# Attention scores with full-height low-part products, and value products in alternating column halves

## The chip, the cores and the metric

The kernel runs on one core of a Trainium2 chip. The metric is the device time of one execution in microseconds (us); lower is better. Engines are named as in the profile: PE (TensorE), PEld (its weight loads), DVE (VectorE), ACT (ScalarE), POOL (GpSimd), SP (SyncE, which issues transfers).

## The reference, cut to what matters

The whole program is two networks, one after the other, on 256 tokens of width 1024. The second one's first layer is an attention with 16 query heads and 4 key heads of width 64. It is computed twice: for 256 context tokens that see themselves, and for the 256 tokens of the sequence, whose keys are the context's and their own (within a window of 128). Each softmax has one extra logit per head, the sink.

```python
def block(n):
    ...
    s_ctx = jnp.einsum('bqgrd,bkgd->bgrqk', qb, kc).astype(F32) * scale
    s_win = jnp.einsum('bqgrd,bkgd->bgrqk', qb, kb).astype(F32) * scale
    s_win = jnp.where(valid, s_win, -jnp.inf)
    p = softmax_with_sink(jnp.concatenate([s_ctx, s_win], axis=-1), sink).astype(v.dtype)
    ...
...
sc = jnp.einsum('bqgrd,bkgd->bgrqk', qc, kc).astype(F32) * scale
pc = softmax_with_sink(sc, sink).astype(vc.dtype)
oc = jnp.einsum('bgrqk,bkgd->bqgrd', pc, vc).reshape(b, C, Q_DIM)
```

## The kernel before, in words

Activations lie with channels on the 128 partitions. Most products split both operands into a high part that PE multiplies in its fast fp32 form (F32R) and a low remainder, and add three products (`mm3`, L185 to L187). Weights stream through a ring of four buffers; ACT makes their high part (L57), DVE the low part (L58).

`attend` (L1405) does one attention. It loops over j (2 pairs of key heads), rp (2 pairs of query heads each) and t (2 blocks of 128 queries), so it has 8 passes of t. In a pass, e is the key head of the pair, and its data lie on partition half `HS[e]`; c is one of two query heads. A pass first makes the scores of four heads (e, c). In the context stage (`nk` is 2: 256 keys) a score is one plain fp32 product on the 64 partitions of its half (L1399); in the main stage (`nk` is 4: 512 keys, two key sets) each is two F32R products per key set (L1402, L1403). For these `q_parts` (L1384) lays the query's high part on half e and its low part on the other half, and `k_parts` (L1332) lays the keys' high part `kh[e]` on both halves; the full-height L1402 thus adds high x high and low x high. The keys' low part `kl` lies on half e alone, so L1403 runs on 64 rows.

Then comes the softmax: mask (main stage, L1431), row maximum (L1434, L1437), exponential on ACT (L1448), the sink's term and the sum (L1449 to L1452), scaling (L1455). After it each head's probabilities are transposed on PE (L1466) into an accumulator bank `ps_pt`, copied by ACT (L1468) into `at`, and multiplied with the values (L1471), which fill the column half `HS[e]` of `po`. All four heads go in the order e, then c; `at` has two buffers in both stages. A plain fp32 product shows as two instructions in the trace, a transpose and an F32R product as one.

PSUM has eight banks in four pools: scores come from `pa` (three), `ps_pt` from `pl` (two). In the main stage `po` has a bank of its own; in the context stage it takes one of the two of `pl`. In the pass with t equal to 1, the next pair's query projection (`q_proj`, L1371, tile `ps_q`) is issued between the softmax and the transposes; its rotary embedding (`rope`, `q_parts`) stands before the last two heads.

The order on each engine is made at build time: a scheduler takes the ready instruction that was written earliest, by its own estimate of durations, so that instructions written later, such as query projections and state tiles, fill waits. On the chip each engine runs that fixed order, and waits where the data isn't there.

After the main stage, `ctx_ssm` (L1664) makes start states of the next layer for groups 1 to 5. Each scales transposed inputs on DVE into the buffer `xd` (L1676 to L1678), which four fp32 products read (L1687). `xd` has `NXD` buffers, two here.

Of the kernel before, what the change touches and what calls it, by code (L numbers as in the profile page):

```python
# [8 lines left out]
F32 = mybir.dt.float32  # L9
F32R = mybir.dt.float32r  # L10
I32 = mybir.dt.int32
AF = mybir.ActivationFunctionType
ALU = mybir.AluOpType

P = 128
S = 256
# [28 lines left out]
HS = slice(0, 64), slice(64, 128)  # L45
# [22 lines left out]
class Core:  # L68
# [25 lines left out]
    TAIL = 4  # L94
    WT = 2
    NXB = 8
    NXD = 2
    UPTO = (6, 11)
    ADA = (1.0, 0.6)
    RATES = (2.4,1.6)  # L100
# [1016 lines left out]
class Second(Core):  # L1117
# [214 lines left out]
    def k_parts(self, kv, name):  # L1332

        nc = self.nc
        kh = [self.w2("%s_h%d" % (name, e), [P, 2, S], F32R) for e in range(2)]
        kl = self.w2(name + "_l", [P, 2, S], F32R)
        for e in range(2):
            for o in (e, 1 - e):
                nc.scalar.copy(kh[e][HS[o]], kv[HS[e]])
            nc.vector.tensor_tensor(kl[HS[e]], kv[HS[e]], kh[e][HS[e]].bitcast(F32), op=ALU.subtract)  # L1340
        return kh, kl

    def kv_proj(self, x, rope, q=None):
# [50 lines left out]
    def scores(self, out, q, k, e, c, j, t, parts):  # L1394

        mm = self.nc.tensor.matmul
        ts = slice(t * P, (t + 1) * P)
        if not parts:
            mm(out, q[HS[e], c, ts], k[HS[e], j], start=True, stop=True)  # L1399
            return  # L1400
        kh, kl = k
        mm(out, q[e][:, c, ts], kh[e][:, j], start=True, stop=False)  # L1402
        mm(out, q[e][HS[e], c, ts], kl[HS[e], j], start=False, stop=True)  # L1403

    def attend(self, x, kvs, rope, out, q):  # L1405

        nc = self.nc
        mm = nc.tensor.matmul
        nk = 2 * len(kvs)
        for j in range(2):  # L1410
            o = self.b4([P, 4, S], F32R, "oh"), self.b4([P, 4, S], F32R, "ol")
            out.append(o)
            for rp in range(2):
                po = self.psum.tile([P, 2, 2, P], F32, tag="pd", name="ps_o2", bufs=1) if rope else self.pl([P, 2, 2, P], "ps_o2")
                i0 = 8 * j + 4 * rp
                for t in range(2):
                    yield
                    mx, sums, nb, es = (self.sm(4, n) for n in ("at_mx", "at_sm", "at_nb", "at_es"))
                    sc = []
                    for e in range(2):  # L1420
                        if nk == 2:
                            pl2 = self.pss([P, 2, S], "ps_s")
                            pl = [pl2[:, c] for c in range(2)]
                        else:
                            pl = [self.pss([P, 512], "ps_s") for _ in range(2)]
                        for c in range(2):
                            for i, kv in enumerate(kvs):
                                self.scores(pl[c][:, i * S:(i + 1) * S], q, kv[0], e, c, j, t, rope)
                            if rope:
                                pb = S + (1 - t) * P  # L1430
                                nc.vector.tensor_tensor(pl[c][:, pb:pb + P], pl[c][:, pb:pb + P], self.amask[:, t], op=ALU.add)  # L1431
                        X = mybir.AxisListType.X
                        if nk == 2:
                            nc.vector.tensor_reduce(mx[:, 2 * e:2 * e + 2], pl2, axis=X, op=ALU.max)  # L1434
                        else:
                            for c in range(2):
                                nc.vector.tensor_reduce(mx[:, 2 * e + c:2 * e + c + 1], pl[c], axis=X, op=ALU.max)  # L1437
                        es_ = slice(2 * e, 2 * e + 2)
                        ks = slice(i0 + 2 * e, i0 + 2 * e + 2)
                        nc.vector.scalar_tensor_tensor(nb[:, es_], mx[:, es_], -0.125, self.nsink[:, ks], op0=ALU.mult, op1=ALU.min)  # L1440
                        if nk == 2:
                            s2 = self.sc([P, 2, S])
                            s_ = [s2[:, c] for c in range(2)]
                        else:
                            s_ = [self.w2("sc", [P, 512], bufs=self.NSC) for _ in range(2)]
                        for c in range(2):
                            k = 2 * e + c
                            nc.scalar.activation(s_[c], pl[c], AF.Exp, bias=nb[:, k:k + 1], scale=0.125, accum_out=sums[:, k:k + 1])  # L1448
                        nc.vector.tensor_tensor(es[:, es_], nb[:, es_], self.sink[:, ks], op=ALU.add)  # L1449
                        nc.scalar.activation(es[:, es_], es[:, es_], AF.Exp)  # L1450
                        nc.vector.tensor_tensor(sums[:, es_], sums[:, es_], es[:, es_], op=ALU.add)
                        nc.vector.reciprocal(sums[:, es_], sums[:, es_])  # L1452
                        for c in range(2):
                            k = 2 * e + c
                            nc.vector.tensor_scalar(s_[c], s_[c], sums[:, k:k + 1], None, op0=ALU.mult)  # L1455
                        sc.append(s_)
                    yield
                    if t == 1 and 2 * j + rp < 3:
                        q = self.q_proj(x, *divmod(2 * j + rp + 1, 2), rope)
                    for e in range(2):  # L1460
                        if e == 1 and t == 1 and 2 * j + rp < 3 and rope:
                            q = self.q_parts(q)
                        for c in range(2):
                            pt = self.pl([P, nk, P], "ps_pt")
                            for kb in range(nk):
                                nc.tensor.transpose(pt[:, kb], sc[e][c][:, kb * P:(kb + 1) * P], self.ident)  # L1466
                            at = self.tl([P, nk, P], name="at") if nk == 2 else self.w2("at", [P, nk, P], bufs=self.NAT)
                            nc.scalar.copy(at, pt)  # L1468
                            for kb in range(nk):
                                g = 2 * j + e  # L1470
                                mm(po[HS[e], c, t], kvs[kb // 2][1][:, kb % 2, g * 64:(g + 1) * 64], at[:, kb], start=(kb == 0), stop=(kb == nk - 1))  # L1471
                yield
                rs = slice(2 * rp, 2 * rp + 2)
                self.split(o[0][:, rs].rearrange("p r s -> p (r s)"), o[1][:, rs].rearrange("p r s -> p (r s)"), po.rearrange("p c t i -> p (c t i)"))
# [189 lines left out]
    def ctx_ssm(self, g):  # L1664
# [8 lines left out]
        for t in range(2):  # L1673
            for c, src in enumerate((xa, xb)):
                te.transpose(px[:, t, c * P:(c + 1) * P], src[:, t * P:(t + 1) * P], self.ident)
        xc = self.w2("xd", [P, 2, 2, S], bufs=self.NXD)  # L1676
        for t in range(2):
# [204 lines left out]
    def run2(self, x, out):  # L1882
# [18 lines left out]
        with ExitStack() as ctx0:  # L1901
# [4 lines left out]
            with ExitStack() as cx:  # L1906
                self.scratch(cx, 1)
                self.pool2 = cx.enter_context(self.tc.tile_pool(name="ssm", bufs=1))
                self.NXB, self.NXD = 12, 1
                self.ssm_setup(self.pool2)  # L1910
# [202 lines left out]
```

## Time and profile before

| | |
|---|---|
| median of 3 runs | 2513.29 us (2512.29 to 2518.58) |
| the profiled execution | 2511.67 us |
| its span, first to last instruction | 2509.7 us |
| mean granted clock of PE in it | 0.975 |

An instruction's line number is that of the kernel before. In a timeline the first number is the start in us from the span's start, the second the duration, and xN the count of like instructions merged into one row. PE is pipelined: an instruction's duration holds a latency that the next one overlaps, so what one costs PE is the step from its start to the next one's.

### The profile page before, as it was taken

To read this page: it belongs to the slowest core of one execution; us is meant where nothing else is said; L and a number is where in the kernel's file an instruction comes from. 1 tells how busy PE (TensorE), PEld (TensorE's weight loads), DVE (VectorE), ACT (ScalarE), POOL (GpSimd) and SP (SyncE) were. 2 spreads that over 40 slices of the span, in tenths; PEclk is the share of its full clock that TensorE was granted. 3 is DMA by queue.
4 is the path that set the end of the run, shared out by engine and by line. 5 is a ranking of instruction groups with operands and counts; after the bars stand their busy time and mean duration, and the time that the engine had idled before them with its cause. 6 is when DMAs were issued, how large, how long until landed. Compare 5 with 4: busy or idle time off the path is not lost.

```text
span 2509.7 us, 49557 instructions
## 1 busy us (share of the span) xinstructions
PE 2359.1 (94%) x19082; PEld 2072.0 (83%) x19082; DVE 1811.0 (72%) x3981; ACT 1234.1 (49%) x2615; POOL 388.9 (15%) x376
## 2 busy tenths in 40 slices
PE   7899999999998999999999999899899989989998
PEld 5787777788888887788988898778799889977997
DVE  7768876677567868687778756856666688985666
ACT  3334435554554444344555455555555556654554
POOL 4210210122013100200012202200200232232000
PEclk8999999999999999999999999899999999999999
DMA  8744563465666654464555666412566644436664
GB/s 243 227 145 148 170 168 85 135 188 186 187 200 195 181 161 140 144 207 146 175 148 179 186 185 198 109 34 85 153 185 183 174 122 126 127 102 205 207 184 130
DMA packets 513005, 404.93 MB, mean 161 GB/s; under 512 B 49969, under 2 KB 445025, under 8 KB 512001
## 3 DMA queue, kind: packets, MB, share of 16 engines
q1 hardware_dynamic: 511536, 397.41, 53.6%
q0 software_dynamic: 1232, 4.36, 0.6%
q8 instruction: 150, 2.46, 0.4%
q14 instruction: 87, 0.70, 0.1%
HBM read 393.19 MB, written 8.52 MB: 160 GB/s over the span
## 4 chain that ended last, share of the span: by engine, by line
PE 70%; DVE 16%; DMA 5%; issue 4%; ACT 4%; POOL 1%; SPq 0%; DVEq 0%; ACTq 0%; POOLq 0%
PE ps_fg L185 4%; PE ps_fg L187 4%; PE ps_fg L186 4%; PE ps_acc L186 4%; PE ps_acc L187 4%; PE ps_acc L185 4%; DVE wl L58 3%; DMA wr<-in_w_in_dram 3%; PE ps_up L187 2%; PE ps_up L186 2%; PE ps_up L185 2%; PE ps_o L1471 2%; PE acc L186 2%; PE acc L187 2%; PE acc L185 2%
## 5 line engine op out<-in xcount | busy, mean ns | idle before, releaser
L57 ACT CAST wh<-wr 128x512 fp32r<-128x512 f32 (+1 forms) x1212 | 741.4, 620 | 808.5 <-PE ps_fg L186 166.6
L58 DVE TENSOR_TENSOR wl<-wr,wh 128x512 fp32r<-128x512 f32 x1092 | 776.5, 719 | 405.6 <-ACT wh L57 398.8
L58 POOL TENSOR_TENSOR wl<-wr,wh 128x512 fp32r<-128x512 f32 (+1 forms) x120 | 160.0, 1352 | 804.1 <-ACT wh L57 789.2
L187 PE MATMUL ps_fg<-xh,wl 128*128 128x256 f32 x672 | 190.2, 283 | 0.0
L186 PE MATMUL ps_fg<-xl,wh 128*128 128x256 f32 x672 | 190.2, 283 | 0.0
L185 PE MATMUL ps_fg<-xh,wh 128*128 128x256 f32 x672 | 190.1, 283 | 0.0
L186 PE MATMUL ps_acc<-wl,hh 128*128 128x512 f32 x432 | 171.6, 397 | 8.9 <-DVE wl L58 8.9
L185 PE MATMUL ps_acc<-wh,hh 128*128 128x512 f32 x432 | 171.0, 396 | 0.0
L187 PE MATMUL ps_acc<-wh,hl 128*128 128x512 f32 x432 | 170.9, 396 | 0.0
L187 PE MATMUL ps_up<-xh,wl 128*128 128x256 f32 x480 | 135.9, 283 | 0.4 <-POOL wl L58 0.4
L185 PE MATMUL ps_up<-xh,wh 128*128 128x256 f32 x480 | 135.8, 283 | 0.0
L186 PE MATMUL ps_up<-xl,wh 128*128 128x256 f32 x480 | 135.8, 283 | 0.0
L185 PEld LDWEIGHTS ps_fg<-xh,wh 128*128 128x128 f32 x672 | 129.0, 192 | 0.4
L186 PEld LDWEIGHTS ps_fg<-xl,wh 128*128 128x128 f32 x672 | 129.0, 192 | 0.4
L187 PEld LDWEIGHTS ps_fg<-xh,wl 128*128 128x128 f32 x672 | 129.0, 192 | 0.0
L186 PEld LDWEIGHTS ps_acc<-wl,hh 128*128 128x128 f32 x432 | 81.8, 189 | 29.4 <-DVE wl L58 12.0
L185 PE MATMUL ps_fg<-ch,wh 128*128 128x256 f32 x352 | 103.1, 293 | 0.6 <-ACT wh L57 0.6
L187 PE MATMUL ps_fg<-ch,wl 128*128 128x256 f32 x352 | 101.4, 288 | 0.0
L186 PE MATMUL ps_fg<-cl,wh 128*128 128x256 f32 x352 | 101.1, 287 | 0.0
L185 PE MATMUL ps_gl<-xh,wh 128*128 128x256 f32 x336 | 99.4, 296 | 0.1
L186 PE MATMUL ps_gl<-xl,wh 128*128 128x256 f32 x336 | 97.9, 291 | 0.0
L187 PEld LDWEIGHTS ps_acc<-wh,hl 128*128 128x128 f32 x432 | 81.7, 189 | 18.9 <-DVE hl L263 0.2
(656 smaller groups left out, 6723.7 us busy)
## 6 DMA issues: line engine op xcount, KB each, us to landing
wr<-in_w_in_dram SPq DMA_DIRECT2D x110, 512.0 KB
adw<-in_ada_w_dram SPq DMA_DIRECT2D x96, 512.0 KB
wr<-in_ssm_w_in_dram SPq DMA_DIRECT2D x72, 512.0 KB
wr<-in_ffn_w_gate_dram SPq DMA_DIRECT2D x66, 512.0 KB
wr<-in_ffn_w_up_dram SPq DMA_DIRECT2D x66, 512.0 KB
wr<-in_ffn_w_down_dram SPq DMA_DIRECT2D x66, 512.0 KB
wr<-in_w_up_dram SPq DMA_DIRECT2D x64, 512.0 KB
wr<-in_w_down_dram SPq DMA_DIRECT2D x64, 512.0 KB
```

What stands on the lines that cost most here:

```text
L57: nc.scalar.copy(hi, raw[:, i:i + self.n])
L58: z = (nc.gpsimd if core.spare > 0 else nc.vector).tensor_tensor(lo, raw[:, i:i + self.n], hi.bitcast(F32), op=ALU.subtract)
L185: mm(out, ah, bh, start=first, stop=False)
L186: mm(out, ah, bl, start=False, stop=False)
L187: mm(out, al, bh, start=False, stop=last)
L1471: mm(po[HS[e], c, t], kvs[kb // 2][1][:, kb % 2, g * 64:(g + 1) * 64], at[:, kb], start=(kb == 0), stop=(kb == nk - 1))
```

## The change

`k_parts` makes the low part for each e on both partition halves, so there are two `kl` tiles per key set instead of one, and two more subtractions per call. The second score product becomes full-height, and so also adds low x low, which was left out before. Room for the tiles is taken from `xd`, which gets one buffer. In the context stage the scores go in the order c, then e, into two accumulators taken together. In both stages the transposes, copies and value products go in the order c, then e, and the value products of the two e are written alternately, after both copies.

```diff
-    NXD = 2
+    NXD = 1
...
-        kh = [self.w2("%s_h%d" % (name, e), [P, 2, S], F32R) for e in range(2)]
-        kl = self.w2(name + "_l", [P, 2, S], F32R)
+        kh, kl = ([self.w2("%s_%s%d" % (name, z, e), [P, 2, S], F32R) for e in range(2)] for z in "hl")
         for e in range(2):
             for o in (e, 1 - e):
                 nc.scalar.copy(kh[e][HS[o]], kv[HS[e]])
-            nc.vector.tensor_tensor(kl[HS[e]], kv[HS[e]], kh[e][HS[e]].bitcast(F32), op=ALU.subtract)
+                nc.vector.tensor_tensor(kl[e][HS[o]], kv[HS[e]], kh[e][HS[e]].bitcast(F32), op=ALU.subtract)
...
         mm(out, q[e][:, c, ts], kh[e][:, j], start=True, stop=False)
-        mm(out, q[e][HS[e], c, ts], kl[HS[e], j], start=False, stop=True)
+        mm(out, q[e][:, c, ts], kl[e][:, j], start=False, stop=True)
...
                     sc = []
+                    if nk == 2:
+
+                        pls = [self.pss([P, 2, S], "ps_s") for _ in range(2)]
+                        for c in range(2):
+                            for e in range(2):
+                                self.scores(pls[e][:, c], q, kvs[0][0], e, c, j, t, rope)
                     for e in range(2):
                         if nk == 2:
-                            pl2 = self.pss([P, 2, S], "ps_s")
+                            pl2 = pls[e]
...
-                            for i, kv in enumerate(kvs):
-                                self.scores(pl[c][:, i * S:(i + 1) * S], q, kv[0], e, c, j, t, rope)
+                            if nk > 2:
+                                for i, kv in enumerate(kvs):
+                                    self.scores(pl[c][:, i * S:(i + 1) * S], q, kv[0], e, c, j, t, rope)
...
-                    for e in range(2):
-                        if e == 1 and t == 1 and 2 * j + rp < 3 and rope:
+                    for c in range(2):
+                        if c == 1 and t == 1 and 2 * j + rp < 3 and rope:
                             q = self.q_parts(q)
-                        for c in range(2):
+                        ats = []
+                        for e in range(2):
                             pt = self.pl([P, nk, P], "ps_pt")
                             for kb in range(nk):
                                 nc.tensor.transpose(pt[:, kb], sc[e][c][:, kb * P:(kb + 1) * P], self.ident)
                             at = self.tl([P, nk, P], name="at") if nk == 2 else self.w2("at", [P, nk, P], bufs=self.NAT)
                             nc.scalar.copy(at, pt)
-                            for kb in range(nk):
+                            ats.append(at)
+
+                        for kb in range(nk):
+                            for e in range(2):
                                 g = 2 * j + e
-                                mm(po[HS[e], c, t], kvs[kb // 2][1][:, kb % 2, g * 64:(g + 1) * 64], at[:, kb], start=(kb == 0), stop=(kb == nk - 1))
+                                mm(po[HS[e], c, t], kvs[kb // 2][1][:, kb % 2, g * 64:(g + 1) * 64], ats[e][:, kb], start=(kb == 0), stop=(kb == nk - 1))
```

## Rows read from the trace of the kernel before

**Rows 1.** The page, part 1: busy time, share of the span, instructions.

```profile
PE 2359.1 (94%) x19082; PEld 2072.0 (83%) x19082; DVE 1811.0 (72%) x3981; ACT 1234.1 (49%) x2615; POOL 388.9 (15%) x376
```

**Rows 2.** The page, part 4: the chain that ended last, by engine.

```profile
PE 70%; DVE 16%; DMA 5%; issue 4%; ACT 4%; POOL 1%; SPq 0%; DVEq 0%; ACTq 0%; POOLq 0%
```

**Rows 3.** Busy time by engine in the main and the context stage.

```profile
core 0: us, PE busy (x) PEld busy (x) DVE busy (x) ACT busy (x) POOL busy (x), PEclk, DMA share, GB/s
1605.00:1738.00 133.00, 132.12 (x841) 105.53 (x842) 85.56 (x225) 71.34 (x170) 6.99 (x5) 1.00 0.23 57
391.00:463.00 72.00, 70.12 (x430) 50.06 (x429) 40.89 (x134) 41.05 (x138) 0.00 (x0) 0.98 0.32 78
```

**Rows 4.** Waits, 1608 to 1735: who waited for whom, us, times, longest.

```profile
DVE ps_s L1431 <- PE ps_s L1403: 29.2, 26, 3.5
...
PEld ps_o L1471 <- ACT z_at L1468: 1.5, 6, 0.3
```

**Rows 5.** Waits, 388 to 466, the context stage.

```profile
DVE at_mx L1434 <- PE ps_s L1399: 11.1, 10, 2.1
...
PEld ps_o L1471 <- ACT at L1468: 6.3, 15, 0.7
```

**Rows 6.** Timeline of PE, 1621.4 to 1628.5 (main stage).

```profile
1621.47 0.39 PE L1402 MATMUL ps_s<-z_kc_h,z_qs 128*128 128x256 f32 x1 [0.29 <-ACT z_sc L1448]
...
1623.98 1.12 PE L1326 MATMUL ps_qp<-q,c_perm 128*128 128x512 f32 x2
...
1625.06 1.04 PE L1466 MATMUL ps_pt<-c_first,z_sc 128*128 128x128 f32 x8
...
1626.34 1.96 PE L1471 MATMUL ps_o<-z_at,kv 128*64 128x128 f32 x16
1628.23 0.38 PE L1402 MATMUL ps_s<-z_kc_h,z_qs 128*128 128x256 f32 x1
```

**Rows 7.** Timeline of PE, 1611 to 1615: query products, full height, same size.

```profile
1614.78 0.28 PE L187 MATMUL ps_q<-xh,wl 128*128 128x256 f32 x1
1614.90 0.28 PE L185 MATMUL ps_q<-xh,wh 128*128 128x256 f32 x1
```

**Rows 8.** Timeline of PE, 1655 to 1672: a short run of value products.

```profile
1661.92 1.09 PE L1471 MATMUL ps_o<-z_at,kv 128*64 128x128 f32 x8
```

**Rows 9.** Timeline of PE, 406.8 to 411.7 (context stage).

```profile
406.87 0.70 PE L1399 MATMUL ps_s<-kv,q 64*128 64x256 f32 x2
407.49 0.65 PE L1471 MATMUL ps_o<-at,kv 128*64 128x128 f32 x4
408.07 0.44 PE L1466 MATMUL ps_pt<-c_first,sc 128*128 128x128 f32 x2
408.44 0.70 PE L1399 MATMUL ps_s<-kv,q 64*128 64x256 f32 x4
409.07 0.65 PE L1471 MATMUL ps_o<-at,kv 128*64 128x128 f32 x4
```

**Rows 10.** Timeline of PE, 394.5 to 396.5: four score instructions of one head.

```profile
394.94 1.13 PE L1399 MATMUL ps_s<-kv,q 64*128 64x256 f32 x4 [0.96 <-ACT sc L1448]
396.00 0.39 PE L186 MATMUL ps_q<-cl,wh 128*128 128x256 f32 x1
```

**Rows 11.** Timeline of PE, 1123.3 to 1124.2: a modulation product in four column groups.

```profile
1123.49 0.64 PE L1160 MATMUL ps_ada<-adw,csc 128*32 128x256 f32 x8
1124.06 0.34 PE L586 MATMUL ps_l<-w_AR,w_Bn 64*64 64x128 f32 x4
```

**Rows 12.** Line 1340, the keys' low part: ns min/median/max, first and last start.

```profile
L1340 DVE TENSOR_TENSOR z_kc_l<-kc,z_kc_h x2: 684/687/690, 1322.9 to 1324.1; 64x512 fp32r<-64x512 f32 x2
L1340 DVE TENSOR_TENSOR z_k_l<-k,z_k_h x2: 677/683/689, 1616.2 to 1618.0; 64x512 fp32r<-64x512 f32 x2
```

**Rows 13.** Groups by line, 1600 to 1740: busy us, mean ns, idle before.

```profile
L1468 ACT COPY z_at<-ps_pt 128x512 f32<-128x512 f32 x32 | 17.1, 589 | 16.1 <-PE ps_pt L1466 16.1
```

**Rows 14.** Timeline of all engines, 1736 to 1751: the buffer xd.

```profile
1738.64 1.46 PE L1687 MATMUL ps_h<-z_xd,cBt 128*128 128x256 f32 x6
...
1740.36 1.29 DVE L1649 TENSOR_TENSOR z_xd<-ps_xct,wctx 128x512 f32<-128x512 f32 x2 [1.66 <-PE ps_xct L1675]
```

## Prediction

> **What bounds the kernel now.** I began with the page: TensorE (PE) is busy for 94% of the span [rows 1], and the chain of work that ended last runs through PE for 70% of it [rows 2]. So work taken off PE can shorten the kernel, if the stage it is taken from is itself held by PE. The change touches two stages, the attention of the context (391 to 463 us) and the main one (1605 to 1738 us). The table by stretches shows what limits each: in the main one PE is busy 132.1 of 133 us, DVE 85.6, ACT 71.3; in the context PE 70.1 of 72, DVE 40.9, ACT 41.1 [rows 3]. The waits say the same from the other side: in the main stage DVE sits 29.2 us until the second score product (L1403) is done, PE's weight loads only 1.5 us for the copied probabilities [rows 4]; in the context DVE waits 11.1 us for scores, and PE's loads 6.3 us for copies, so there PE is already partly held by the chain [rows 5]. Last, the timeline of PE, read by starts and not by durations: the time from one start to the next is what an instruction costs PE, its duration holds pipeline latency too.
>
> **The change part by part.**
>
> *Scores, main stage.* Today a full-height product (L1402) alternates with one on 64 rows (L1403). Eight of them take 1621.47 to 1623.98, 2.51 us, 0.314 us each [rows 6]. A full-height product of the same 256 columns in a stream of its like starts 0.12 us after the one before [rows 7]. The change makes every second product full-height, so the stream never changes its shape: 128 products (8 passes of t, 4 heads, 2 key sets, 2 products) x 0.194 = 24.8 us. Some already stand next to products of their own height, so I take 23 (estimate).
>
> *Values, main stage.* A run of 16 instructions, which is two heads in one column half (each fp32 product is two instructions, and L1471 has 256 of them for 128 products), takes PE 1.89 us, from 1626.34 to 1628.23 [rows 6]. A run of eight is 0.87 shorter, 1.96 against 1.09 [rows 8], so it costs 1.02. The passes show one run of 16 and two of eight: 3.93 us, 31.4 over 8 passes. After the change each pass has two runs of 8 + 8 in the two column halves. No row shows 64-wide column halves side by side. The nearest is the modulation product, in four column groups of 32 and also two instructions per product: its eight instructions take 0.57 us from start to the next engine start [rows 11], while two 256-column instructions in one place, one after the other, take 0.63 [rows 9]. Four groups thus cost no more than one. With that, 16 instructions cost little more than a run of eight, 1.02; I take 1.06, 17.0 over the stage's 16 runs: 14.4 saved. The bounds: 0 if the halves don't overlap, 14.4 if they do fully. I take 14.4, the modulation product being the same kind of packing.
>
> One rule speaks against this. The Trainium skill, page "TensorE: Matmul & The Clock Gate", section "What overlaps and what doesn't", says that a weight load overlaps with running products only when its row group differs; the two column halves share all their rows. By that rule this saving would be about 0, as in the first rival below. [rows 11] disagree with it.
>
> *Values, context.* A run of four costs 0.58 us (407.49 to 408.07) [rows 9], 32 runs, 18.6 us. Joined in pairs, 16 runs at a little more, 0.61: 9.8, so 8.8 saved.
>
> *Scores, context.* Four instructions in both row halves cost 0.63 us (408.44 to 409.07), as much as two in one half (406.87 to 407.49) [rows 9], while four in one half cost 1.06 [rows 10]. So row halves do overlap, and PE does it today wherever the two happen to be adjacent. Per two passes of t today: five such runs at 0.63, 3.15 us, 12.6 over the stage. After: each pass all eight in pairs, 1.06 (the row of four singles, doubled up), 8.5. Saved 4.1.
>
> In sum PE loses 37.4 us of work in the main stage and 12.9 in the context, 50.3.
>
> *What of it reaches the end, main.* With 132.1 - 37.4 = 94.7 us of PE work left, DVE's 85.6 comes close, and the softmax between scores and values alternates DVE and ACT. No row shows this stage with DVE so loaded. Bounds: it could follow PE fully (95 us, DVE at 0.90) or stay where DVE is used as now, 0.64, and gain nothing. I take DVE at 0.82, nearer to the full end because DVE's largest waits there are the 29.2 us for the products that shrink: (85.6 + 1.4) / 0.82 = 106 us, a gain of 27. The transfers won't hold it up: the DMA share there is 0.23 [rows 3].
>
> *What reaches the end, context.* Transposes and the accumulator share two PSUM buffers here, so the second head's transposes wait until the first head's copy has read the buffer, and now the values wait for both copies. Bounds 0 and 12.9; PE already waits there [rows 5], so I take half, 6.5.
>
> *Added subtractions.* Each call of k_parts gets two more on half the partitions, 0.683 us each [rows 12]. The context keys' pair is made at 1323 [rows 12], 280 us ahead of the stage that reads it. The own keys' pair stands just ahead of the first scores, where PE has query products to run: between 0 and 1.4, taken as 1.4 (also in the 87 above).
>
> *One xd buffer instead of two.* The next group's scaling (L1649) must now wait until the last group's products are through. It does so already: the products that read the buffer start their last run at 1738.64 and the next scaling starts at 1740.36, just when its own input is transposed [rows 14]. Cost 0; if groups overlapped more, at most 1.29 us per group, 6.5 for five.
>
> *Added waits.* The values of the first head wait for the copy of the second, 0.589 us later [rows 13]; behind them in PE's queue stand the next scores, and the next copies wait for the two probability buffers, both held until the pair is through. In the main stage the next pass's scores and query products cover this; without that cover it costs 0.59 x 16 = 9.4.
>
> Sum: -27 - 6.5 + 1.4 + 0 = -32. The profiled execution took 2511.7 (span 2509.7), 1.6 below the median of 2513.3: 2481 us as a median.
>
> **The rivals.**
> *Column halves don't overlap.* For it: the column halves share rows, and the scheduler may put all of one head's values first. Against: [rows 11]. Then PE frees 23 in the main stage (110 us left, above the 106) and 4.1 in the context, half of it felt: -23 - 2 + 1.4, 2490. Chance 0.15.
> *The softmax chain takes over early.* DVE can't be filled beyond 0.70 because both heads' softmax stands before the first values: 87 / 0.70 = 124 us, -9, context 0, +1.4: 2506. For it: PE's loads in the context wait for copies already [rows 5]. Against: DVE's own waits end mostly with PE. Chance 0.12.
> *Everything freed is felt.* -50, 2463, if queries and the context's next work fill each gap. Chance 0.10.
> *Lost overlap, slower.* Today the first head's transposes, copies and values run while the second head's softmax is on DVE. Afterwards no values run until both are done, and only two probability buffers exist. If this phase lies bare, each pair costs eight transposes (1.04) [rows 6], two copies (2 x 0.589) [rows 13] and its values (1.06), 3.3 us, 52 over the 16 pairs, against 37.4 freed; with 1.4 for the subtractions and the context taken as even, +16: 2529. It decides from 4.7 us of bare wait per main pass (37.4 / 8); today it is 1.5 us in the whole stage [rows 4]. Chance 0.08.
>
> **How the numbers follow.** The forecast of a 32 us gain has 0.55, its own range 2471 to 2494 (DVE share 0.76 to 0.88, context 0 to 10). The range for all runs from full effect (2463) to the early chain (2505), leaving out the slower case and part of the early chain. About 0.3%, 7.5 us, is what a measurement can tell from no change, so below 2506 is faster: the forecast, the full case, the column rival and a third of the chain case, 0.84; within 0.3% 0.08; slower 0.08.
>
> **What the changed profile would show.** Right: the L1402/L1403 products start 0.12 us apart, with the weight load of L1403 on 128 rows; the values' instructions start in pairs some 10 ns apart and 16 of them take about 1.06 us; the main stage is near 106 us with DVE above 0.8 and DVE's wait for scores well under 29 us, PE's wait for DVE or ACT grown to some 10 us; the context stage near 66 us. Wrong: values still at 0.11 us each; PE idle of over 4.7 us per main pass before transposes or values; DVE share as before at a shorter PE; or a gain there that comes back as a wait for weights or in the state groups after 1735.

## The result, and the profile after

The changed kernel took 2483.13 us (median of four runs, 2480.52 to 2488.66), the kernel before 2515.88 beside it: a ratio of 0.9874, 95% interval 0.985 to 0.9898, so 32.7 us faster. Measured a second time it took 2479.57 against 2511.0: 0.9885, interval 0.9862 to 0.9908. Its profiled execution took 2480.52 us, with a span of 2478.6 and a mean granted clock of 0.974.

The page of the changed kernel, part 1, which answers to [rows 1]:

```profile
PE 2327.0 (94%) x19082; PEld 2050.7 (83%) x19082; DVE 1813.5 (73%) x3985; ACT 1235.4 (50%) x2615; POOL 388.4 (16%) x376
```

PE lost 32 us of busy time, as much as the whole kernel became shorter, and its weight loads 21; DVE, ACT and POOL kept theirs within 2.5 us. The instruction counts of PE are the same; DVE has the four subtractions more. Where the time went is read by stretches. The next two fences give the main stage from its first score product to its last value product, before and after; the columns are those of [rows 3], with all instructions in the first row, then only those that touch the scores' accumulators, the value products' and the query projection's (`ps_s`, `ps_o`, `ps_q`). Before:

```profile
1611.20:1733.80 122.60, 121.72 (x765) 95.86 (x764) 78.39 (x212) 65.01 (x158) 5.70 (x4) 1.00 0.22 57
1611.20:1733.80 122.60, 40.37 (x128) 23.49 (x128) 31.02 (x64) 23.66 (x64) 1.00 0.22 57
1611.20:1733.80 122.60, 32.78 (x255) 27.23 (x256) 2.08 (x3) 1.76 (x3) 1.00 0.22 57
1611.20:1733.80 122.60, 24.87 (x144) 18.96 (x144) 0.00 (x0) 1.76 (x3) 1.00 0.22 57
```

After:

```profile
1608.80:1702.10 93.30, 89.82 (x755) 76.57 (x754) 80.13 (x214) 65.61 (x158) 5.76 (x4) 1.00 0.27 69
1608.80:1702.10 93.30, 23.11 (x128) 17.53 (x128) 30.26 (x64) 23.75 (x64) 1.00 0.27 69
1608.80:1702.10 93.30, 24.01 (x255) 16.53 (x256) 2.06 (x3) 1.75 (x3) 1.00 0.27 69
1608.80:1702.10 93.30, 22.16 (x144) 18.74 (x144) 0.00 (x0) 1.76 (x3) 1.00 0.27 69
```

The stage is 29.3 us shorter, nearly the whole gain. PE's busy time in it fell by 31.9: 17.3 for the scores, 8.8 for the values, 2.7 for the query products, which nobody touched, and 3.2 for the rest. The stage has ten instructions fewer, all of them state products (`ps_xbc`, 96 before, 86 after) that now run elsewhere, so some 2 us of the 29.3 are moved and not saved. PE still fills 96% of the stage, and DVE 80.1 of 93.3 us, 0.86. The waits of the same stage, which answer to [rows 4]:

```profile
DVE ps_s L1437 <- PE ps_s L1402: 5.2, 6, 1.7
...
PEld ps_o L1481 <- ACT z_at L1475: 2.0, 8, 0.4
```

DVE's wait for scores shrank from 29.2 to 5.2 us, and the weight loads wait hardly more for the copied probabilities, 2.0 us against 1.5. The timeline of PE shows the two edits at work, and one flaw (x14 stands for 14 instructions in one row):

```profile
1620.08 0.28 PE L1402 MATMUL ps_s<-z_kc_l,z_qs 128*128 128x256 f32 x1
1620.20 0.28 PE L1401 MATMUL ps_s<-z_k_h,z_qs 128*128 128x256 f32 x1
1620.32 0.28 PE L1402 MATMUL ps_s<-z_k_l,z_qs 128*128 128x256 f32 x1
...
1623.21 0.43 PE L1481 MATMUL ps_o<-z_at,kv 128*64 128x128 f32 x2
1623.57 0.39 PE L187 MATMUL ps_q<-xh,wl 128*128 128x256 f32 x1
...
1628.78 1.09 PE L1481 MATMUL ps_o<-z_at,kv 128*64 128x128 f32 x14
1629.80 0.66 PE L1473 MATMUL ps_pt<-c_first,z_sc 128*128 128x128 f32 x4
```

Score products now follow each other at 0.12 us whether high or low part, where [rows 6] had 0.314. Of the 16 instructions of a value run, two go alone ahead of the rest (here by 5.6 us, elsewhere in the stage by 0.7 to 3.8): the first head's first product, ready as soon as its own copy is. The other 14 take 1.02 us to the next start; most of them begin in pairs 7 ns apart. All 16 value runs of the stage look like this.

The context stage, first score to last value product, with all instructions, scores, values. Four profiles have the context in the order of before. In three of them (the kernel before and two experiments below, from 396.6, 398.0 and 393.2) the granted clock stands at 0.5 for 3.4 us of the stage, and it takes about 70.7 us. I take the fourth, the experiment on xd below, where it stands at 1.00 throughout:

```profile
394.40:463.60 69.20, 67.31 (x422) 47.88 (x422) 40.47 (x133) 40.09 (x135) 0.00 (x0) 1.00 0.32 80
394.40:463.60 69.20, 13.62 (x64) 6.60 (x64) 11.04 (x16) 17.34 (x64) 1.00 0.32 80
394.40:463.60 69.20, 20.52 (x127) 13.03 (x128) 2.04 (x3) 1.78 (x3) 1.00 0.32 80
```

The changed kernel:

```profile
393.60:461.40 67.80, 67.35 (x425) 46.39 (x424) 38.89 (x133) 40.40 (x136) 0.00 (x0) 1.00 0.34 83
393.60:461.40 67.80, 15.99 (x64) 8.03 (x64) 10.76 (x16) 16.64 (x64) 1.00 0.34 83
393.60:461.40 67.80, 17.08 (x128) 9.60 (x128) 2.05 (x3) 1.76 (x3) 1.00 0.34 83
```

Only 1.4 us came of it, and none of that is work taken off PE, which is busy for 67.3 us in both. The values lost 3.4 us of PE time, but the scores cost 2.4 more. The timeline says why:

```profile
407.41 0.43 PE L1481 MATMUL ps_o<-at,kv 128*64 128x128 f32 x2
407.77 0.70 PE L1398 MATMUL ps_s<-kv,q 64*128 64x256 f32 x2
408.40 0.65 PE L1481 MATMUL ps_o<-at,kv 128*64 128x128 f32 x6
408.98 0.44 PE L1473 MATMUL ps_pt<-c_first,sc 128*128 128x128 f32 x2
```

A value run is broken into 2 + 6, for 0.36 and 0.58 us to the next start, and two score instructions go alone for 0.63, the price of four in both row halves [rows 9].

### The profile page after: what moved, and what is told of

It reads as the page before. It is cut to its first block, busy times and chain, and to the rows that moved or that the text cites. A ratio compares the mean times of both kernels' runs of the same rounds, so it can differ in the third digit from the quotient of the medians.

```text
span 2478.6 us, 49551 instructions
## 1 busy us (share of the span) xinstructions
PE 2327.0 (94%) x19082; PEld 2050.7 (83%) x19082; DVE 1813.5 (73%) x3985; ACT 1235.4 (50%) x2615; POOL 388.4 (16%) x376
## 4 chain that ended last, share of the span: by engine, by line
PE 69%; DVE 17%; DMA 5%; issue 4%; ACT 4%; POOL 1%; SPq 0%; ACTq 0%; DVEq 0%; POOLq 0%
PE ps_fg L185 5%; PE ps_fg L187 4%; PE ps_fg L186 4%; PE ps_acc L186 4%; PE ps_acc L187 4%; PE ps_acc L185 4%; DVE wl L58 4%; DMA wr<-in_w_in_dram 3%; PE ps_up L187 2%; PE ps_up L186 2%; PE ps_up L185 2%; PE acc L185 2%; PE acc L186 2%; PE acc L187 2%; PE ps_o L1481 2%
## 5 line engine op out<-in xcount | busy, mean ns | idle before, releaser
L186 PEld LDWEIGHTS ps_acc<-wl,hh 128*128 128x128 f32 x432 | 81.6, 189 | 27.8 <-DVE wl L58 10.3
```

Source lines behind the costliest of these rows:

```text
L186: mm(out, ah, bl, start=False, stop=False)
```

## The experiments

All times are medians; each ratio is to the kernel before on the same chip.

**Scores alone.** The changed kernel with the value order, and the order of the context scores, as before.

```diff
-                    for c in range(2):
-                        if c == 1 and t == 1 and 2 * j + rp < 3 and rope:
+                    for e in range(2):
+                        if e == 1 and t == 1 and 2 * j + rp < 3 and rope:
...
```

> The change with its order of scores and values undone: only the full-height second score product of the main stage (and one xd buffer) is left. The main stage, first score product to last value product, took 122.6 us before and 93.3 with the whole change. Theory (PE held the main stage, and each of the two parts frees its own PE time; with both, DVE at 0.84 takes back some 8 us): the scores alone free 23, the stage takes 99 to 102 us, the run is 20 to 23 us faster than before, the values stay at 0.109 us an instruction. Rival (the chain of softmax and copies holds the stage, and it is the new order of the values that loosened it): the stage stays above 110 us and the gain below 12. The context stage stays at 70 to 71 us in both.

2497.42 us, ratio 0.9935, interval 0.9912 to 0.9959. Main stage, all instructions, scores, query products:

```profile
1612.60:1716.50 103.90, 100.32 (x766) 88.73 (x764) 79.57 (x214) 65.06 (x158) 5.75 (x4) 1.00 0.26 66
1612.60:1716.50 103.90, 22.80 (x128) 17.56 (x128) 30.47 (x64) 23.81 (x64) 1.00 0.26 66
1612.60:1716.50 103.90, 23.25 (x144) 18.99 (x144) 0.00 (x0) 1.75 (x3) 1.00 0.26 66
```

The stage shrinks by 18.7 us, for 21.4 less of PE's busy time, 17.6 of it the scores': nearly all that PE loses, the stage loses, so PE held it. The rival (above 110 us) is out. The theory's sizes were too large: a stage of 99 to 102 us, and 20 to 23 us off the run, where the ratio gives 16.

**Values alone.** The kernel before with the new order of transposes, copies and value products in both stages, and nothing else.

```diff
-                    for e in range(2):
+                    for c in range(2):
...
+                        for kb in range(nk):
+                            for e in range(2):
```

> The kernel before with only the new order of transposes, copies and values, in both stages; scores and keys' parts as before. Theory (PE time freed counts): the values' instructions start in pairs 7 ns apart, main stage 14 us shorter, 108 to 110 us, the run 13 to 18 us faster. If the two parts simply add, this and the scores alone give about 29; if DVE takes part of it back when both are there, their sum is 34 to 38. Rival (both heads' copies before the first value product make a new wait): main stage 115 us or more, gain under 8, PE's waits for the copies (2.0 us in the whole main stage with the change) above 5.

2502.96 us, ratio 0.9962, interval 0.9947 to 0.9977. All instructions, scores and values of its main stage:

```profile
1605.30:1720.50 115.20, 114.36 (x746) 86.18 (x744) 78.31 (x210) 65.29 (x156) 5.70 (x4) 0.96 0.22 56
1605.30:1720.50 115.20, 40.18 (x128) 23.56 (x128) 30.84 (x64) 23.97 (x64) 0.96 0.22 56
1605.30:1720.50 115.20, 24.12 (x256) 16.63 (x256) 2.08 (x3) 1.76 (x3) 0.96 0.22 56
```

The stage is 7.4 us shorter. Two things blur that. This execution had a mean granted clock of 0.96 in it (three stretches of 3.4 us at 0.5, the lower level of 1.2 GHz), which is worth some 3 x 1.7 = 5 us (half of each). And 20 of the 96 state products have moved out of the stage, some 3 us of PE time. With both set right it is some 9 us shorter (an estimate), about what the values lost of PE time, 8.7 (8.8 in the full change). The two halves of the change then give -18.7 - 9 = -28, against -27 for both at once with its ten moved products set right in the same way: they add, as far as two profiles can show it. In the whole time they give 0.65% and 0.38%, against 1.26% and 1.15% for the full change, which adds too within the intervals. The gain here, 8.4 us, is below the theory's 13 to 18; the rival's sign, waits for the copies above 5 us, did not come, PE's loads wait 1.3 us for them in the stage.

**Is it DVE that holds the rest?** The changed kernel without the 32 mask additions (the window isn't applied).

```diff
-                            if rope:
-                                pb = S + (1 - t) * P
-                                nc.vector.tensor_tensor(pl[c][:, pb:pb + P], pl[c][:, pb:pb + P], self.amask[:, t], op=ALU.add)
```

> The change without the mask's addition in the main stage (32 additions of 0.30 us on DVE, 0.21 us each from start to start, left out, so the window is not applied). With the change DVE is busy 84.9 of 101 us there and PE 97.5. Theory (DVE and its chain took back about 8 of the 37 us freed on PE): the stage is 5 to 8 us shorter than the 93.3 us of the change. Rival (PE still holds it): 0 to 2 us shorter.

2480.03 us, ratio 0.9873, interval 0.9846 to 0.9899, the changed kernel's own. The main stage, and DVE's largest wait for scores in it:

```profile
1604.80:1696.90 92.10, 88.65 (x747) 75.11 (x746) 71.90 (x181) 65.45 (x157) 6.09 (x4) 1.00 0.27 70
```

```profile
DVE at_mx L1440 <- PE ps_s L1402: 10.3, 15, 1.9
```

With 8.2 us less on DVE the stage is 1.2 us shorter, with eight state products fewer in it, and DVE spends the freed time waiting for PE, 10.3 us instead of 5.2. DVE at 0.86 doesn't hold this stage; PE does.

**The values one head after the other, behind both copies.**

```diff
-                        for kb in range(nk):
-                            for e in range(2):
+                        for e in range(2):
+                            for kb in range(nk):
```

> The change with its value products written one head after the other, all four key blocks of the first head and then those of the second, still behind both copies. Theory (what counts is that products of both column halves stand next to each other in PE's queue; the context scores before, written two and two per half, already started in pairs): pairs 7 ns apart as with the change, main stage 92 to 95 us, run within 4 us of it. Rival (the products must be written alternately): instructions 0.109 us apart, main stage 8 to 14 us longer, run 10 to 18 us slower than the change.

2496.18 us, ratio 0.994, interval 0.992 to 0.996, some 14 to 17 us above the changed kernel: the theory (within 4 us) fell. The main stage takes 100.5 us, 7.2 more than in the changed kernel though 18 more of its state products run elsewhere, and the context stage 71.4, 3.6 more. Most value runs of the main stage are of eight, one head alone; five times both heads' stand together as 16:

```profile
1641.45 1.09 PE L1481 MATMUL ps_o<-z_at,kv 128*64 128x128 f32 x8
1642.47 1.12 PE L1326 MATMUL ps_qp<-q,c_perm 128*128 128x512 f32 x2
...
1678.95 1.07 ACT L1475 COPY z_at<-ps_pt 128x512 f32<-128x512 f32 x2 [0.47 <-PE ps_pt L1473]
...
1680.06 1.58 PE L1481 MATMUL ps_o<-z_at,kv 128*64 128x128 f32 x16
1681.57 0.39 PE L185 MATMUL ps_xbc<-ch,wh 128*128 128x256 f32 x1
```

Eight instructions of one head cost 1.02 us, what 14 of both cost in the changed kernel. But this kernel lost two things at once: the alternation, and mostly the neighbourhood too, since the scheduler issues the first head's eight as soon as its copy is done. The run at 1680.06 has the neighbourhood alone: both copies had ended at 1680.02, and the 16 take 1.51 us. That is more than 1.02 and less than two times 1.02: the second head's first instruction starts 0.49 us after the run's first, together with the first head's fifth. So here an unbroken run that isn't written in turn brings about half. Another experiment, further down, parts the two for runs of four and four.

**The context part undone.** The changed kernel with the context stage in the order of before.

```diff
+                    if nk == 2:
+                        for e in range(2):
+                            for c in range(2):
...
+                    else:
                     for c in range(2):
```

> The changed kernel with the context stage's scores, transposes, copies and values in the order of the kernel before; the main stage stays changed. Theory (the context part brought little, since the pairs mostly don't form there): the context stage goes back from 67.8 to 69 to 71 us, the kernel is 1 to 3 us slower than the changed one, near 2483 to 2486. Rival (the prediction's term): 6.5 us come back, the stage takes 73 to 75, the kernel near 2489.

2481.2 us, ratio 0.9887, interval 0.987 to 0.9904; the changed kernel has 0.9874 and 0.9885. The context part of the change can't be seen in the whole time; the prediction's 6.5 us for it aren't there. The context stage takes 70.7 us, with 3.4 us at the lower clock in it, as the theory had it (69 to 71); the main stage is the same.

**One bank and one copy in the context.** The changed kernel, but both heads' transposes of the context go into one bank, and one copy takes both.

```diff
+                        if nk == 2:
+                            pt = self.pl([P, 2, nk, P], "ps_pt")
+                            for e in range(2):
+                                for kb in range(nk):
+                                    nc.tensor.transpose(pt[:, e, kb], sc[e][c][:, kb * P:(kb + 1) * P], self.ident)
+                            at = self.tl([P, 2, nk, P], name="at")
+                            nc.scalar.copy(at, pt)
+                            ats = [at[:, e] for e in range(2)]
...
```

> The changed kernel, but in the context stage both heads' transposes go into one accumulator bank and one copy takes both (512 columns, 0.59 us by the main stage's copies, for two of 0.37). Theory (the context's gain was lost because the second head's transposes wait for the bank and the first head's first value product then goes alone): all 64 instruction pairs of values form there instead of 32, PE's values take some 10 us of starts instead of 15, PE's and ACT's waits on that bank shrink, and the stage takes 62 to 65 us. Rival (the stage is held by the softmax chain, not by PE and the bank): 67 to 68 us, as in the changed kernel.

2471.75 us, ratio 0.9851, interval 0.9834 to 0.9868. The context stage, all instructions, scores, values, and a value run in its timeline:

```profile
392.90:450.50 57.60, 56.98 (x424) 43.15 (x423) 37.65 (x133) 38.01 (x120) 0.00 (x0) 1.00 0.37 94
392.90:450.50 57.60, 14.07 (x64) 7.88 (x64) 10.89 (x16) 17.00 (x64) 1.00 0.37 94
392.90:450.50 57.60, 10.26 (x128) 6.64 (x128) 2.05 (x3) 1.75 (x3) 1.00 0.37 94
```

```profile
401.14 0.66 PE L1489 MATMUL ps_o<-at,kv 128*64 128x128 f32 x8
401.73 0.66 PE L1474 MATMUL ps_pt<-c_first,sc 128*128 128x128 f32 x4
```

Both heads become ready at one moment, so all eight instructions run as one, 0.59 us, and the stage shrinks by 10.2 us, more than the theory's 3 to 6: besides the values' 6.8 us of PE time the scores got 1.9 cheaper and the transposes 2.1 (13.4 to 11.3), since their four go as one run too. PE is busy for 99% of the stage with one copy and without: it was PE and its order, not the softmax chain.

**The order of the context scores.** The one-copy version with the scores as before, head half after head half.

```diff
-                        for c in range(2):
-                            for e in range(2):
-                                self.scores(pls[e][:, c], q, kvs[0][0], e, c, j, t, rope)
...
+                            for i, kv in enumerate(kvs):
+                                self.scores(pl[c][:, i * S:(i + 1) * S], q, kv[0], e, c, j, t, rope)
```

> The one-copy version with the context scores in the order of the kernel before (head half after head half, each into its accumulator). Theory (the order written doesn't decide, since the accumulators come free one after the other, and as many score pairs form either way): the stage stays at 57 to 58.5 us and the time within 1.5 us of the one-copy version's. Rival (the prediction's: the order c, then e saves about 4 us of PE work): the stage takes 60 to 62.

2471.15 us, ratio 0.9849, interval 0.9821 to 0.9877. Its context stage, all instructions, then scores:

```profile
396.30:455.20 58.90, 57.15 (x422) 43.27 (x423) 38.11 (x133) 38.06 (x120) 0.00 (x0) 1.00 0.37 94
396.30:455.20 58.90, 14.10 (x64) 7.94 (x64) 10.99 (x16) 17.08 (x64) 1.00 0.37 94
```

The scores cost the same 14.1 us in either order; the stage is 1.3 us longer, a little more than the theory allowed, and nothing of it shows in the time. The order written was worth none of the 4.1 us on PE that I gave it.

**Alternation or neighbourhood?** The one-copy version, with the context's values written one head after the other. Here both are ready at once, so the run stays whole.

```diff
-                        for kb in range(nk):
-                            for e in range(2):
+                        for kb, e in [(kb, e) for e in range(2) for kb in range(nk)] if nk == 2 else [(kb, e) for kb in range(nk) for e in range(2)]:
+                            if True:
```

> The one-copy version with the context's value products written one head after the other: the same instructions, still in one uninterrupted run of eight, but four in one column half and then four in the other, not alternating. Theory (two instructions overlap only if they lie in different column halves and stand next to each other): few pairs start together, a run of eight costs 1.0 to 1.15 us instead of 0.59, PE's values 16 to 18 us instead of 9.4, and the stage takes 62 to 66 us. Rival (an uninterrupted run is what helps, not the alternation): the stage stays at 57.6.

2471.57 us, ratio 0.9854, interval 0.983 to 0.9878. The context stage, all instructions, and a run:

```profile
388.90:446.60 57.70, 57.09 (x424) 43.27 (x423) 37.63 (x133) 38.03 (x120) 0.00 (x0) 1.00 0.35 94
```

```profile
402.28 0.67 PE L1489 MATMUL ps_o<-at,kv 128*64 128x128 f32 x8
402.88 0.66 PE L1474 MATMUL ps_pt<-c_first,sc 128*128 128x128 f32 x4
```

My theory fell. Four instructions in one column half followed by four in the other take 0.60 us, as little as the alternating run and as four of one half alone [rows 9]. The rival held, at this length: an unbroken run of four and four needs no alternation. For eight and eight, unbroken wasn't enough (1.51 us, above).

**One xd buffer.** The kernel before with `NXD = 1`.

```diff
-    NXD = 2
+    NXD = 1
```

> The kernel before with one xd buffer instead of two, and nothing else. Theory: no change, 2511 to 2514, and the time from the end of the main stage to the end of the span stays within 1 us. Rival: the next group's scaling is late by its own 1.29 us in each of five groups, 6.5 us slower, 2518 to 2520.

2510.44 us against 2509.35, ratio 1.0006, interval 0.9994 to 1.0018: nothing. The timeline answers to [rows 14], where the same two starts also lie 1.72 us apart:

```profile
1737.14 1.46 PE L1687 MATMUL ps_h<-z_xd,cBt 128*128 128x256 f32 x6
...
1738.86 1.29 DVE L1649 TENSOR_TENSOR z_xd<-ps_xct,wctx 128x512 f32<-128x512 f32 x2 [1.66 <-PE ps_xct L1675]
```

**The context keys' subtractions on POOL.**

```diff
-                nc.vector.tensor_tensor(kl[e][HS[o]], kv[HS[e]], kh[e][HS[e]].bitcast(F32), op=ALU.subtract)
+                eng = nc.gpsimd if name == "kc" and o != e else nc.vector
+                eng.tensor_tensor(kl[e][HS[o]], kv[HS[e]], kh[e][HS[e]].bitcast(F32), op=ALU.subtract)
```

> The changed kernel with the two added subtractions of the context keys on POOL instead of DVE. Theory (they stand ahead of the weights' low parts on DVE at 1322 us, and PE waits for those): PE's wait for the weights' low part at 1318 to 1330 goes back from 2.4 to about 1.0 us, and the work behind it starts 1.4 to 2.6 us earlier. Rival (they are covered, and the longer wait there comes from something else, a clock dip or the order): the wait stays at 2.4 and nothing starts earlier. In the whole time either is too small to show surely; the trace decides.

2478.82 us, ratio 0.9891, interval 0.9872 to 0.9909: nothing to see in the time. What counts is how long PE's weight load waits here for the low part of a weight, which DVE makes behind these subtractions. In the three profiles without the added pair it waits 0.6 us (values alone), 0.8 (one xd buffer) and 1.2 (the kernel before); in the nine that have it on DVE 1.7 to 2.6, 2.1 in the mean; with POOL doing it 2.0 here and 1.8 in the next experiment's kernel. The kernel before, the changed kernel's second profile, and the next experiment's kernel:

```profile
PEld ps_xbc L187 <- DVE wl L58: 1.2, 1, 1.2
```

```profile
PEld ps_xbc L187 <- DVE wl L58: 1.7, 1, 1.7
```

```profile
PEld ps_xbc L187 <- DVE wl L58: 1.8, 1, 1.8
```

The added pair costs some 1.2 us (the means, 2.1 against 0.9), and moving it to POOL gives almost nothing back. I expected 1.4 to 2.6 back. The timeline of the last of the three says why:

```profile
1310.18 3.43 POOL L1340 TENSOR_TENSOR z_kc_l<-kc,z_kc_h 64x512 fp32r<-64x512 f32 x2 [2.47 <-ACT z_kc_h L1338]
...
1311.35 1.11 DVE L1340 TENSOR_TENSOR z_kc_l<-kc,z_kc_h 64x512 fp32r<-64x512 f32 x1 [0.59 <-ACT z_kc_h L1338]
...
1312.49 1.66 DVE L263 TENSOR_TENSOR xl<-m,xh 128x512 fp32r<-128x512 f32 x1
```

Beside POOL's two, DVE's second subtraction takes 1.11 us, where it takes 0.69 alone [rows 12], and the next one 1.66, where it takes 0.69 in the changed kernel: most of what DVE was spared, it loses again.

**A version that beats both, beside the changed kernel on the same chip.** One copy in the context, and the subtractions on POOL.

> The changed kernel again, unaltered, as the measure for the three that follow on the same chip. Both theories: some 1.2% below the kernel before.

> The changed kernel with one bank and one copy for both heads in the context stage, and the added subtractions of the context keys on POOL. Theory (the two gains add): 10 us less than the changed kernel from the context stage and 0.6 at 1322 us, some 2470 to 2473 where the changed one takes 2481, faster than both kernels. Rival (what the shorter context stage gives is given back later, as the first profile of the one-copy version with its 3.7 us suggests): 2477 to 2480.

The changed kernel took 2479.57 us (ratio given at the top), this one 2474.65, ratio 0.9865, interval 0.9844 to 0.9887: 4.9 us less, between the two expectations. Its context stage is 57.6 us again. The four kernels with one copy have ratios of 0.9849 to 0.9865, mean 0.9855; the changed kernel, its repetition and the two that differ from it by the context's order or the keys' subtractions alone have 0.9874 to 0.9891, mean 0.9884. The difference, 0.0029, is 7 us: one copy beats both kernels. Whether the 3 us missing from the stage's 10.2 are given back later stays open; the stretches at the lower clock lie elsewhere in each execution and cover about as much. The POOL part isn't worth keeping.

## Why the prediction was right

The time, 2483.1, lies 2 us from the 2481.0 forecast, and what the forecast rests on came true: PE held the main stage, the scores' stream keeps its shape, the column halves overlap. The terms fared less well. The forecast gave 33.5 us to the two stages, where 30.7 came, and the closeness is in part luck, errors that cancel. With some 1.2 us against them for the subtractions, about 3 of the 32.7 us stand in no stage looked at here; the interval is 26 to 38.

**Scores, main: the mechanism right, the size a quarter too large.** The stream keeps its shape and runs at 0.12 us. I took 23 us off PE; adding up the steps from start to start over the stage gives 37.4 before and 18.7 after, 18.7 off. That is 0.29 and 0.15 a product, where I had 0.314 and 0.12. A score product that follows a transpose, a value or a permutation product costs 0.2 to 0.4 us (0.23 at 1632.79, 0.40 at 1619.68).

**Values, main: right that the halves overlap, wrong on the run.** I priced 16 instructions as one run of 1.06 us. It is 14 for 1.02 and two alone for 0.36 (the rows above), 1.38 in all, and 22.1 over the 16 runs instead of 17.0: 9.3 us saved, not 14.4. The step that failed is the assumption that the first product waits for both copies because it is written behind both; only the second head's products do.

**What reaches the end, main: the size near, the limiter wrong.** I let DVE, at a share of 0.82, hold a window of 133 us [rows 3] at 106. The same window of the changed kernel, with the same margins around the stage, takes 103.7, and DVE fills 0.83 of it:

```profile
1602.60:1706.30 103.70, 100.22 (x828) 86.06 (x829) 86.19 (x224) 70.48 (x166) 7.05 (x5) 1.00 0.30 75
```

Both numbers came near, but not for my reason: taking 8 us off DVE moved the stage by 1.2, so DVE's share was no limit. PE held it, and nearly all that was freed on PE was felt, 29.3 of 31.9; PE idles 3.5 us in the stage, not the 10 that I named as a sign. Too much freed (37.4), and too little let through (27), gave 27 where 29.3 was measured. That is luck.

**Context: the term of 6.5 was mis-sized, 1.4 came.** Bounded from 0 to 12.9, I took half because PE waited there. What failed is the 12.9 itself, not the half: PE's busy time in the stage did not fall (67.31 before, 67.35 after), since value runs and score runs were broken and the scores even cost 2.4 us more. With the value runs whole, PE lost 10.4 us of busy time and the stage 10.2.

**Subtractions:** the sum had 1.4 for the own keys' pair and 0 for the context's. The context's cost some 1.2, because behind them on DVE stand the low parts of weights for which PE waits; I had looked only at their reader, 280 us later. For the own keys' pair no run was made, so its 1.4 is not shown. **xd:** 0, as forecast, shown alone.

**The rivals.** That column halves don't overlap is refuted by 14 instructions in 1.02 us against eight of one half in 1.02. The rule of the Trainium skill ("TensorE: Matmul & The Clock Gate", section "What overlaps and what doesn't"), by which a weight load overlaps only products of another row group, would have meant 2490; this trace disagrees with it, the two halves having the same rows. The early softmax chain needed DVE stuck at 0.70, and it reached 0.83 in the window of [rows 3]. The slower case needed 4.7 us of bare wait per main pass; PE's loads wait 2.0 us for copies in the whole stage [rows 4: 1.5]. The case in which everything is felt described the main stage best; it missed the time because less was freed, in the context nothing.

## What to carry to other kernels

Before pricing an array packing by its instructions, ask when each of them becomes ready: a scheduler that issues what is ready first breaks a run that the code writes whole, and one shared buffer with one copy, which makes both halves ready together, was worth several times as much here as the order written. Writing the halves in turn brought nothing where one half's run was four instructions long; with eight, an unbroken run that was not in turn cost half a microsecond more. Price a small instruction by what stands behind it on its own engine, not only by who reads its result, and before moving it to another engine look at what that engine's work does to its neighbour. And where PE is the bound, at 99%, another engine's share before says little about its limit: DVE went from 0.64 to 0.86 here and still held nothing. Compare a forecast with the trace over the window that it was made for.

## What the runs showed of the hardware that was not expected

PE runs products of two column halves side by side even when they aren't written in turn: 0.60 us for four of one half and then four of the other, 0.58 for four alone. So the second half's products start before the first half's last ones: on PE the order given at build time is not the order in which products start. The Trainium skill ("TensorE: Matmul & The Clock Gate", section "What overlaps and what doesn't") says that products start strictly in the order issued; this run disagrees with that too. One run of the heads-in-turn kernel shows how far this went with eight of one half and then eight of the other. Both copies were done at 1680.02, but the second half's first product started only at 1680.55, together with the first half's fifth; in the run of four and four it started 14 ns after the first. Whether the distance sets this, or the wait for a copy of its own that the second half has in the longer run and not in the shorter, no run separates.

A 64-row product between full-height ones costs time in its neighbours as well: with the scores alone changed, the query products, which nobody touched, took 1.6 us less of PE (24.87 to 23.25). In the full change it is 2.7, and the rest goes with other neighbours that changed too.

DVE's subtractions became slower beside POOL's: 1.11 and 1.66 us instead of 0.69, and 1.12 and 1.66 in the run with POOL alone changed.

The granted clock falls to its lower level, 0.5, for stretches of mostly 3.4 us, some of them inside stages in which PE is busy throughout, at other places in each execution. One such stretch made the context stage of before 70.7 us instead of 69.2, so it is worth 1.5 to 1.7 us (half of 3.4). Such stretches stood in stages that an edit touches in the kernel before (396.6) and in three experiments: scores alone (398.0), the context undone (393.2), and values alone (three in the main stage).
